# A hybrid encoder step on one core: another order of instructions in the attention step and in the opening

## The chip, the cores and the metric

The kernel runs on one core of one Trainium2 chip. The metric is the device time of one execution in microseconds (us). Before the change the median of three runs was 1349.14 us (1349.07 to 1354.99).

## What is computed

One layer of a streaming encoder, for a prompt of 1024 tokens and a running stream of 32 new tokens with 512 cached ones; the width is 1024, with 16 heads of 64. Everything is float32. Cut to what matters here:

```python
h = rmsnorm(x, norm_g)
q, k = rmsnorm(h @ Wq) * 64**-0.5, rmsnorm(h @ Wk)      # per head
v, logf = h @ Wv, log_sigmoid(h @ Wf + b_f)
u = (h @ Wua) * sigmoid(h @ Wub)
ga, gb, ma, mb = h @ Wga, h @ Wgb, h @ Wma, h @ Wmb
c = cumsum(logf)
p = softmax(where(causal, q @ k.T + c_q - c_k, -inf))   # per head, 128 queries at a time
o = p @ v
conv = causal_depthwise_conv(u, w_dw, 31 taps) + b_dw
ya = (o * silu(ga)) @ Wpa
yb = (silu(layernorm(conv)) * silu(gb)) @ Wpb
y = x + (sigmoid(ma) * ya + sigmoid(mb) * yb) @ Wout
```

Outputs are y, k, v, logf and the last 30 rows of u for both streams.

## The kernel before, in words

All data stands transposed: channels on the 128 partitions, the 1056 tokens along the free axis. A projection's output tile is 128 channels; its product runs over 8 k-tiles, in three chunks of 352 tokens. To keep float32 accuracy in 16-bit matmuls, the input and each weight tile are split into a high and a low part (`xh`, `xl`; `wh`, `wl`), and each product is three matmuls (`mms`, L183). Splitting a weight is: its squares for the scale on ACT (`stage`, L117), a sum over partitions on PE (`total`), a power of two (`power`), the high part on ACT (`high`, L138) and the low part on DVE in three pieces (`low`, L141). These jobs are due at fixed counts of `beat`, which is called once for each k-tile of a product (`begin`). A beat also adds `pace["rate"]` to a credit, from which the convolution's taps (`conv_taps`, L371, one DVE instruction over 1086 columns for each of 31 taps of 8 channel tiles) are issued.

**Opening** (`x_split`, L550 and after). The tokens come in three chunks of 256, 384 and 416. For each chunk and k-tile PE transposes the tokens (`ptx`, L576), ACT makes `xh` (L578) and DVE `xl` (L579). A table of jobs by k-tile says what else is issued there: squares of the next tokens, their roots (`rooted`, then `steps_of[...]`: two activations and a few small DVE operations), the scaling of the tokens (`scale`, L541 on DVE, L539 on GpSimd) and the parts of the first two weight tiles (`high(i, p)`, `low(i, p)`: part p of tile i). The products of the two tiles stand behind the transposes by a lag: `drain((2, 5))` in the first chunk, `drain((2, 2))` in the others.

**Attention.** A list `seq` holds 16 heads of 8 blocks (128 queries against all keys so far) and 4 `Sample` steps, one for four heads of the cached stream each. The step for element n in the loop at L1244 and after issues work of several elements:

- `scores` of n+3: two or four matmuls into PSUM (`psS`, L1121 and L1122; two buffers of two banks), then on DVE an add of the mask to the diagonal (L1124) and a maximum (`nm`, L1126).
- `turn` of n: the normalized weights `P` are transposed on PE (`ptr`, L1153) in groups of four into tiles of the pool `psT`, which has two buffers. The first group is copied out by ACT, the second (blocks 4 to 7) by DVE (`pt`, L1156).
- `soft` of n+3: the exponential on ACT (L1133), with its sum.
- `norm` of n+2: a reciprocal on DVE (L1138), then a scaling on GpSimd (L1139).
- `values` of n-2: with a head's last block 40 matmuls into two tiles of `psT` (`po`, L1172), copied and added into `ot` by ACT (L1176) and DVE (L1177, and L1179 with the gate `ga` for odd heads); for a `Sample` its own products.
- `fill(k)`: k steps of pending gate projections (`filler`), each the three matmuls of one k-tile, with a beat. There are 22 weight tiles of 24 steps, 528 steps in all.
- One step of `layernorm`, once the convolution's sums are there (`sides["ready"]`): sums over channels on PE into a tile of `psT` (`psn`, L1202), a scaling of the mean on ACT (L1211), the square of the mean (L1215) and three DVE operations (L1216 to L1218), later roots.

PE, SP, DVE and ACT keep the order in which the program issues here; only GpSimd is ordered by a planner. Loads of a head's `QA`, `QB`, `KA`, `KB` (L960 and after), of `ga` and of cache blocks go through SP's queue in that order too.

After the attention come the output products, which the change doesn't touch.

Of the kernel before, what the change touches and what calls it, by code (L numbers as in the profile page):

```python
# [8 lines left out]
F32 = mybir.dt.float32  # L9
# [5 lines left out]
ALU = mybir.AluOpType  # L15
AX = mybir.AxisListType

D = 1024
T = 1024
# [6 lines left out]
CH = 352  # L26
# [4 lines left out]
LNO = ((0,), (1, 2), (3,), (4, 5), (6,), (7,), ())  # L31
LNEXP = "natural_log_exp_and_others"
NFILL = 22
R_U, R_V, R_QK, R_G, R_A = 0.21, 0.18, 0.165, 0.23, 0.2
NWARM = 34
HT = TT // 2
HC = HT // 2
# [16 lines left out]
def build(tc, xT, xt, wv, wf, ckT, cv, clT, stT, vec, cst, yT, kT, vO, lfO, cpT, csT):  # L54
    nc = tc.nc
# [3 lines left out]
    def pool(name, bufs=1, stack=es, **kw):  # L59
        return stack.enter_context(tc.tile_pool(name=name, bufs=bufs, reuse_waits="tile", **kw))  # L60
# [19 lines left out]
    rstd = lnp.tile([128, TT], F32, name="rstd")  # L80
# [9 lines left out]
    class Batch:  # L90
# [46 lines left out]
        def high(self, i, wh, raw, ks):  # L137
            nc.scalar.mul(wh[:, ks, :], raw[:, ks, :], self.s[:, i:i + 1])  # L138

        def low(self, i, wl, wh, raw, ks):  # L140
            nc.vector.scalar_tensor_tensor(wl[:, ks, :], raw[:, ks, :], self.s[:, i:i + 1], wh[:, ks, :],  # L141
                                           op0=ALU.mult, op1=ALU.subtract)
# [35 lines left out]
    def mms(ps, w, rh, rl, sl, kts=range(KT), first=True, last=True):  # L178
        wh, wl = w[:2]
        n, N = 0, 3 * len(kts)  # L180
        for kt in kts:
            for a, b in ((wh, rh), (wl, rh), (wh, rl)):
                nc.tensor.matmul(ps, a[:, kt, :], b(kt, sl), start=(first and n == 0), stop=(last and n == N - 1))  # L183
                n += 1

    def csl(c):
        return slice(c * CH, (c + 1) * CH)
# [95 lines left out]
    class Banks:  # L283

        n = 0
# [101 lines left out]
    def pieces(o, n):  # L387

        if o + n <= T:
            return ((slice(0, n), slice(30 + o, 30 + o + n)),)  # L390
        return ((slice(0, T - o), slice(30 + o, 30 + T)), (slice(T - o, n), slice(60 + T, 60 + T + TS)))
# [134 lines left out]
    def root(t0, nt):  # L526

        rs = rs9[:, t0:t0 + nt]
        v, y = [xip.tile([128, 4], F32, name=f"n4{i}", tag=f"n4{i}", bufs=2)[:, :nt] for i in range(2)]
        nc.vector.tensor_scalar(v, rs, 1.0 / D, EPS, op0=ALU.mult, op1=ALU.add)  # L530
        nc.scalar.activation(y, v, AF.Ln)
        nc.scalar.activation(y, y, AF.Exp, scale=-0.5)
        return lambda: newton(rs, v, y)

    def scale(t, h, pool=False):
        r = rows(t)
        x, f = xtok[t][:r, half[h]], rs9[:r, t:t + 1]
        if pool:
            nc.gpsimd.tensor_scalar(x, x, f, 1.0, op0=ALU.mult, op1=ALU.mult)  # L539
        else:  # L540
            nc.vector.tensor_scalar(x, x, f, None, op0=ALU.mult)  # L541
# [3 lines left out]
    def drain(lags):  # L545
        for q, n in zip(behind, lags):
            while len(q) > n:
                q.pop(0)()

    def x_split(c, ws, u, jobs):  # L550


        o, n = XCH[c]
        sl = slice(o, o + n)
        pss = [pj.tile([128, 512], F32, name="pj", tag="pj") for _ in range(2)]

        def project(i, kt):
            mms(pss[i][:, :n], ws[i], X, XL, sl, range(kt, kt + 1), kt == 0, kt == KT - 1)
            if kt < KT - 1:
                return  # L560
            if i == 0:
                for a, b in pieces(o, n):
                    nc.scalar.mul(u[:, b], pss[0][:, a], recs[0].inv)
                return
            nc.vector.tensor_scalar(ua0[:, sl], pss[1][:, :n], recs[1].inv, None, op0=ALU.mult)
            if c == 2:
                for o2, n2, a2 in PCS:
                    b = slice(30 + o2, 30 + o2 + n2)
                    nc.scalar.activation(u[:, b], u[:, b], AF.Sigmoid)
                    nc.vector.tensor_mul(u[:, b], ua0[:, a2:a2 + n2], u[:, b])  # L570

        for kt in range(KT):
            pt = tr.tile([128, 512], F32, name="ptx", tag="tr") if kt % 3 == 2 else st.tile([128, 512], F32, name="ptx", tag="st")
            for j in range((n + 127) // 128):
                r = min(128, n - 128 * j)
                nc.tensor.transpose(pt[:, 128 * j:128 * j + r],  # L576
                                    xtok[o // 128 + j][:r, 128 * kt:128 * kt + 128], ident[:r, :r])
            nc.scalar.mul(xh[:, kt, sl], pt[:, :n], gs[:, kt:kt + 1])  # L578
            nc.vector.scalar_tensor_tensor(xl[:, kt, sl], pt[:, :n], gs[:, kt:kt + 1], xh[:, kt, sl],  # L579
                                           op0=ALU.mult, op1=ALU.subtract)  # L580
            for job in jobs.get(kt, ()):
                job()
            for i in range(2):
                behind[i].append(lambda i=i, kt=kt: project(i, kt))
            drain((2, 5 if c == 0 else 2))

    u0 = u_tile(0)
    ua0 = xip.tile([128, TT], F32, name="ua0")
# [13 lines left out]
    def known(i):  # L602
        recs[i].power(psq[:, i + 1:i + 2], 1)
# [19 lines left out]
    steps_of = {}  # L623

    def rooted(t0, nt):
        steps_of[t0] = root(t0, nt)
# [12 lines left out]
    for f in range(8):  # L639
# [16 lines left out]
        1: [lambda: squares(3)],  # L656
        2: [lambda: high(0, 1), lambda: low(0, 1)],
        3: [lambda: total(2), lambda: known(1), lambda: squares(4)],
        4: [lambda: high(1, 0), lambda: low(1, 0), lambda: rooted(2, 3), lambda: high(0, 2)],
        5: [lambda: steps_of[2](), lambda: scale(2, 0), lambda: scale(3, 0, True), lambda: scale(4, 0), lambda: low(0, 2)],  # L660
        6: [lambda: scale(3, 1, True), lambda: scale(2, 1), lambda: high(1, 1), lambda: low(1, 1)],
        7: [lambda: scale(4, 1), lambda: high(1, 2), lambda: low(1, 2)]})
    x_split(1, ws0, u0, {
# [73 lines left out]
    for c in range(4):  # L737
# [16 lines left out]
        for t in range(8):  # L754
            ps = pj.tile([128, 512], F32, name="pjv", tag="pj")
            n = 0
            for kt in range(KT):
                sl = slice(t * 128, t * 128 + 128)
# [243 lines left out]
    psT = pool("psT", 2, stack=p2, space=PS)  # L1002
# [4 lines left out]
    class Two:  # L1007
        n = 0
# [14 lines left out]
    def fill(n):  # L1023
        for _ in range(n):
            next(flow, None)
# [157 lines left out]
    seq = []  # L1183
# [12 lines left out]
    def pending(b):  # L1196
        return isinstance(b, Sample) or b.i % 2

    def over_channels(acc, put):
        for c in range(3):  # L1200
            pm = psT.tile([128, 512], F32, name="psn", tag="T")
            nc.tensor.matmul(pm[:, :CH], ones_f, acc[:, csl(c)], start=True, stop=True)  # L1202
            put(csl(c), pm[:, :CH])
            yield

    def layernorm():

        shift = sides["shift"]
        for _ in range(4):
            yield  # L1210
        yield from over_channels(mean, lambda sl, ps: nc.scalar.mul(mean[:, sl], ps, 1.0 / D))  # L1211

        def put(sl, ps):
            t = t352("t", 3)
            nc.scalar.activation(t, mean[:, sl], AF.Square)  # L1215
            nc.vector.scalar_tensor_tensor(rstd[:, sl], ps, 1.0 / D, t, op0=ALU.mult, op1=ALU.subtract)  # L1216
            nc.vector.tensor_add(mean[:, sl], mean[:, sl], shift[:, sl])
            nc.vector.tensor_scalar(rstd[:, sl], rstd[:, sl], EPS, None, op0=ALU.add)  # L1218

        yield from over_channels(rstd, put)  # L1220
        for c in range(6):
            sl = slice(c * CH // 2, c * CH // 2 + CH // 2)
            v, y = rstd[:, sl], t352("t", 3)[:, :CH // 2]
            nc.scalar.activation(y, v, AF.Ln)
            nc.scalar.activation(y, y, AF.Exp, scale=-0.5)
            yield
            w = t352("t", 3)[:, :CH // 2]
            nc.vector.tensor_copy(w, v)
            newton(v, w, y)
            yield  # L1230

    ones_f = cp.tile([128, 128], F32, name="ones_f", tag="ob")
# [5 lines left out]
    for n in range(3):  # L1238
# [3 lines left out]
            seq[n - 1].norm()  # L1242
        fill((8, 4, 0)[n])
    for n, b in enumerate(seq):  # L1244
        if n + 3 < len(seq):
            start(seq[n + 3])
        if n + 9 < len(seq) and getattr(seq[n + 9], "i", 1) == 0:
            seq[n + 9].head.load()
        if n + 6 < len(seq) and isinstance(seq[n + 6], Sample):
            seq[n + 6].load()  # L1250
        if getattr(b, "i", 0) == 3 and b.head.h + 1 < H:
            heads[b.head.h + 1].load_v()
        b.turn()
        if n + 3 < len(seq):
            seq[n + 3].soft()
        if n + 2 < len(seq):
            seq[n + 2].norm()
        some = 2 if isinstance(b, Sample) or b.i > 2 or b.head.h != 8 else 0
        fill(some)
        if n >= 2 and pending(seq[n - 2]):  # L1260
            seq[n - 2].values()
        fill(some)
        if n >= 3 and isinstance(seq[n - 3], Sample):
            seq[n - 3].finish()
        if "ready" in sides:
            next(ln, None)
# [17 lines left out]
    class Banks3:  # L1284
        n = 0
# [383 lines left out]
```

## Time and profile before

| what | value |
|---|---|
| median of three runs | 1349.14 us (1349.07 to 1354.99) |
| the profiled execution | 1345.89 us |
| its span, first to last instruction | 1344.1 us |
| granted TensorE clock in it, mean | 0.996 |
| PE idle in the first 60 us | 5.5 us |
| PE idle in the attention, 565.9 to 1052.6 us | 21.1 us |

The profile is of one execution. A row of a timeline gives start and duration in us, engine, line, operation, what it writes and reads, and in brackets the idle time of the engine before it with what ended it. A row of waits gives who waited for whom, the sum in us, how often, and the longest. A row of windows gives the stretch, its length and the busy time of PE, weight loads, DVE, ACT and GpSimd (POOL), each with its number of instructions, then the mean granted clock, the share of DMA and GB/s. A row of the chain gives start, length and what was on the path that ended last.

### The profile page before, as it was taken

The page shows a single profiled execution, that of the slowest core. Times are in us where ns is not written, and L with a number is a line of the kernel's source. Part 1 is how long each engine was busy: PE and PEld are TensorE (multiplying, and loading weights), DVE is VectorE, ACT ScalarE, POOL GpSimd, SP SyncE. Part 2 cuts the span into 40 slices and gives each one's busy share as a digit, 9 for nine tenths or more (in the row PEclk, how much of TensorE's full clock was granted, in tenths as well). Part 3 has the DMA queues.
Part 4 walks back from the last instruction along what each step waited for, and adds up shares of the span by engine and source line. Part 5 has one row for each costly group of instructions (what it writes and reads, how often), then busy time and mean ns, then how long its engine had stood idle before and what let it go on. Part 6 is the DMA issues. An engine that isn't in the chain of part 4 may idle for free.

```text
span 1344.1 us, 24837 instructions
## 1 busy us (share of the span) xinstructions
PE 1312.6 (98%) x9383; PEld 1003.1 (75%) x9383; DVE 990.4 (74%) x1532; ACT 719.0 (53%) x1362; POOL 505.8 (38%) x548
## 2 busy tenths in 40 slices
PE   8999999999999999999889998999999999999999
PEld 5687876666666666667567766777776699999998
DVE  6797879888999997987778866655554489166664
ACT  6644555757676743455555555655555566233320
POOL 2001124547484820243433442222222158255562
PEclk8999999999999999999999999999999999999999
DMA  6343233425352463535644643565452698544462
GB/s 251 98 140 104 93 112 118 139 82 187 95 180 87 162 166 109 160 90 155 165 109 123 186 132 99 147 179 132 131 152 54 240 313 262 176 128 146 142 190 69
DMA packets 113496, 194.97 MB, mean 145 GB/s; under 512 B 34080, under 2 KB 80032, under 8 KB 113376
## 3 DMA queue, kind: packets, MB, share of 16 engines
q1 hardware_dynamic: 113232, 193.31, 46.9%
q8 instruction: 74, 1.21, 0.4%
q14 instruction: 46, 0.38, 0.1%
q10 hardware_dynamic: 144, 0.07, 0.0%
HBM read 127.68 MB, written 65.64 MB: 144 GB/s over the span
## 4 chain that ended last, share of the span: by engine, by line
PE 82%; DVE 9%; ACT 3%; issue 2%; DMA 2%; SPq 1%; POOL 0%; DVEq 0%; ACTq 0%; POOLq 0%
PE pj L183 56%; PE pjv L761 6%; PE pj L1501 6%; PE po L1172 4%; PE ptr L1153 3%; DVE nm L1126 2%; DVE wl L141 2%; DVE y L371 2%; PE psS L1122 2%; PE psS L1121 2%; DMA ga<-s_ga 2%; ACT wh L138 1%; DVE psS L1124 1%; DMA s_q<-qh 1%; PE warm L477 1%
## 5 line engine op out<-in xcount | busy, mean ns | idle before, releaser
L183 PE MATMUL pj<-xh,wh 128*128 128x352 f16 (+2 forms) x1536 | 481.6, 314 | 2.3 <-ACT wh L138 1.4
L183 PE MATMUL pj<-xh,wl 128*128 128x352 f16 (+2 forms) x1536 | 481.2, 313 | 0.7 <-DVE wl L141 0.6
L183 PE MATMUL pj<-xl,wh 128*128 128x352 f16 (+2 forms) x1536 | 480.9, 313 | 0.5 <-DVE xl L579 0.4
L183 PEld LDWEIGHTS <-wh 128*128 128x128 f16 x3072 | 301.5, 98 | 162.1 <-issue 7.1
L371 DVE SCALAR_TENSOR_TENSOR y<-u,vec_t,y 128x1086 f32<-128x1086 f32 x240 | 346.8, 1446 | 12.0 <-ACT y L368 8.9
L1139 POOL TENSOR_SCALAR P<-P,nm 128x128 f32<-128x128 f32 (+7 forms) x128 | 129.9, 1015 | 279.9 <-DVE nm L1138 229.8
L183 PEld LDWEIGHTS <-wl 128*128 128x128 f16 x1536 | 150.5, 98 | 72.0 <-DVE wl L141 1.6
L141 DVE SCALAR_TENSOR_TENSOR wl<-raw,sc,wh 128x384 f16<-128x384 f32 (+1 forms) x192 | 128.2, 693 | 48.3 <-ACT wh L138 48.3
L1133 ACT ACTIVATE P<-psS,nm 128x128 f32<-128x128 f32 (+7 forms) x128 | 95.1, 743 | 113.3 <-DVE nm L1138 70.9
L1126 DVE TENSOR_REDUCE nm<-psS 128x1 f32<-128x128 f32 (+7 forms) x128 | 97.0, 758 | 12.5
L1153 PE MATMUL ptr<-ident,P 128*128 128x128 f32 x576 | 88.6, 276 | 17.3 <-DVE pt L1156 9.2
L175 POOL TENSOR_TENSOR wl<-raw,wh 128x384 fp32r<-128x384 f32 (+1 forms) x51 | 63.3, 1270 | 74.3 <-ACT wh L172 58.6
L1153 PEld LDWEIGHTS ptr<-ident,P 128*128 128x128 f32 x576 | 69.2, 141 | 28.2 <-DVE pt L1156 12.1
L1156 ACT COPY pt<-ptr 128x512 f32<-128x512 f32 (+3 forms) x128 | 64.3, 502 | 44.4 <-PE ptr L1153 43.2
L1121 PE MATMUL psS<-KB,QB 128*128 128x256 f32 (+2 forms) x192 | 81.8, 427 | 0.6 <-ACT P L1133 0.6
L880 POOL TENSOR_TENSOR sql<-sqf,sqh 128x352 fp32r<-128x352 f32 x48 | 57.0, 1187 | 65.8 <-ACT sqh L877 65.8
L138 ACT ACTIVATE wh<-raw,sc 128x1024 f16<-128x1024 f32 (+1 forms) x68 | 73.9, 1091 | 8.2 <-DVE sc L158 7.9
L1172 PE MATMUL po<-pt,V 128*64 128x256 f32 x640 | 72.8, 382 | 2.5 <-ACT pts L1078 1.7
L1124 DVE TENSOR_TENSOR psS<-psS,cmask 128x128 f32<-128x128 f32 x128 | 37.6, 294 | 46.0 <-PE psS L1122 45.6
L906 POOL TENSOR_TENSOR ql<-qn,qh 128x352 fp32r<-128x352 f32 (+1 forms) x48 | 67.8, 1429 | 6.6 <-ACT qh L905 6.5
L761 PE MATMUL pjv<-vwh,xh 128*128 128x260 f16 x256 | 70.1, 274 | 0.0
L761 PE MATMUL pjv<-vwl,xh 128*128 128x260 f16 x256 | 70.0, 273 | 0.0
(271 smaller groups left out, 2532.9 us busy)
## 6 DMA issues: line engine op xcount, KB each, us to landing
raw<-wf SPq DMA_DIRECT2D x92, 512.0 KB
QB<-s_q SPq DMA_DIRECT2D x32, 256.0 KB
KB<-s_k SPq DMA_DIRECT2D x32, 256.0 KB
kT<-qn SPq DMA_DIRECT2D x8, 528.0 KB
s_ga<-t SPq DMA_DIRECT2D x24, 176.0 KB
s_gb<-t SPq DMA_DIRECT2D x24, 176.0 KB
s_ma<-t SPq DMA_DIRECT2D x24, 176.0 KB
s_mb<-t SPq DMA_DIRECT2D x24, 176.0 KB
```

Source lines behind the costliest of these rows:

```text
L138: nc.scalar.mul(wh[:, ks, :], raw[:, ks, :], self.s[:, i:i + 1])
L141: nc.vector.scalar_tensor_tensor(wl[:, ks, :], raw[:, ks, :], self.s[:, i:i + 1], wh[:, ks, :], op0=ALU.mult, op1=ALU.subtract)
L183: nc.tensor.matmul(ps, a[:, kt, :], b(kt, sl), start=(first and n == 0), stop=(last and n == N - 1))
L371: t = nc.vector.scalar_tensor_tensor(y, u[:, i:i + CW], w, y, op0=ALU.mult, op1=ALU.add)
L761: nc.tensor.matmul(ps[:, :VC], a, b, start=(n == 0), stop=(n == 23))
L1121: nc.tensor.matmul(ps[:, b, :wm], QB[:, qsl], KB[:, ksl], start=True, stop=False)
L1126: nc.vector.tensor_reduce(nm[:, 0:1], ps[:, :nb, :w], axis=AX.XY, op=ALU.max, negate=True)
L1133: nc.scalar.activation(P[:, :nk].rearrange("p (b w) -> p b w", b=nb), ps[:, :nb, :w], AF.Exp, bias=nm[:, 0:1], accum_out=nm[:, 1:2])
L1139: nc.gpsimd.tensor_scalar(P[:, :nk], P[:, :nk], nm[:, 2:3], 1.0, op0=ALU.mult, op1=ALU.mult)
L1153: nc.tensor.transpose(pt[:, 128 * j:128 * j + 128], P[:, 128 * (4 * u + j):128 * (4 * u + j) + 128], ident)
L1172: nc.tensor.matmul(po[rows], V[:, j, :], parts[c][:, j, :], start=(c % 2 == 0 and j < 2), stop=(c % 2 == 1 and j >= 2 * c))
L1501: nc.tensor.matmul(pss[c][:, :HC], a[:, k, :], x, start=(not more and kt == 0 and n == 0), stop=(kt == 3 and n == 2), skip_group_check=more)
```

## The change

Five edits. The taps' rate in the attention goes from 0.2 to 0.165 a beat. In the opening the second tile's products lag seven k-tiles, and the jobs of k-tiles 4 and 5 change places. In `layernorm` the square of the mean is issued one step ahead of the matmul that it belongs to. In the attention's step `turn` of n and `norm` of n+2 come first, then the scores of n+3 and the loads, then the values of n-2, the exponential of n+3 and all fills together. The fills are four for each step, three at block 6 of heads 2 to 13; before, they were two and two around the values, and none at the first three blocks of head 8.

```diff
-R_U, R_V, R_QK, R_G, R_A = 0.21, 0.18, 0.165, 0.23, 0.2
+R_U, R_V, R_QK, R_G, R_A = 0.21, 0.18, 0.165, 0.23, 0.165
...
-            drain((2, 5 if c == 0 else 2))
+            drain((2, 7 if c == 0 else 2))
...
-        4: [lambda: high(1, 0), lambda: low(1, 0), lambda: rooted(2, 3), lambda: high(0, 2)],
-        5: [lambda: steps_of[2](), lambda: scale(2, 0), lambda: scale(3, 0, True), lambda: scale(4, 0), lambda: low(0, 2)],
+        4: [lambda: rooted(2, 3), lambda: high(0, 2), lambda: steps_of[2](), lambda: scale(2, 0), lambda: scale(3, 0, True)],
+        5: [lambda: scale(4, 0), lambda: high(1, 0), lambda: low(0, 2), lambda: low(1, 0)],
...
-        def put(sl, ps):
+        for c in range(3):
+            sl = csl(c)
             t = t352("t", 3)
             nc.scalar.activation(t, mean[:, sl], AF.Square)
-            nc.vector.scalar_tensor_tensor(rstd[:, sl], ps, 1.0 / D, t, op0=ALU.mult, op1=ALU.subtract)
+            yield
+            pm = psT.tile([128, 512], F32, name="psn", tag="T")
+            nc.tensor.matmul(pm[:, :CH], ones_f, rstd[:, sl], start=True, stop=True)
+            nc.vector.scalar_tensor_tensor(rstd[:, sl], pm[:, :CH], 1.0 / D, t, op0=ALU.mult, op1=ALU.subtract)
...
-        yield from over_channels(rstd, put)
...
     for n, b in enumerate(seq):
+        b.turn()
+        if n + 2 < len(seq):
+            seq[n + 2].norm()
         if n + 3 < len(seq):
             start(seq[n + 3])
...
-        b.turn()
+        if n >= 2 and pending(seq[n - 2]):
+            seq[n - 2].values()
         if n + 3 < len(seq):
             seq[n + 3].soft()
-        if n + 2 < len(seq):
-            seq[n + 2].norm()
-        some = 2 if isinstance(b, Sample) or b.i > 2 or b.head.h != 8 else 0
-        fill(some)
-        if n >= 2 and pending(seq[n - 2]):
-            seq[n - 2].values()
-        fill(some)
+        fill(3 if getattr(b, "i", 0) == 6 and 2 <= b.head.h < 14 else 4)
```

## The prediction, made before the result was known

> **What bounds the kernel now.** I read the page's engine line and the shares of its chain first, then busy time by stage, then who PE (the matmul engine) waited for in the attention, then single stretches of PE, DVE (VectorE) and ACT (ScalarE).
>
> ```profile
> PE 1312.6 (98%) x9383; PEld 1003.1 (75%) x9383; DVE 990.4 (74%) x1532; ACT 719.0 (53%) x1362; POOL 505.8 (38%) x548
> ...
> PE 82%; DVE 9%; ACT 3%; issue 2%; DMA 2%; SPq 1%; POOL 0%; DVEq 0%; ACTq 0%; POOLq 0%
> ```
> ```profile
> 0.00:20.00 20.00, 16.37 (x80) 10.19 (x81) 11.18 (x40) 13.42 (x30) 4.50 (x14) 0.83 0.94 348
> 20.00:60.00 40.00, 38.13 (x252) 24.94 (x251) 30.50 (x62) 24.77 (x45) 3.81 (x6) 1.00 0.30 102
> 565.90:820.00 254.10, 239.85 (x1777) 173.04 (x1777) 191.76 (x372) 142.75 (x308) 97.99 (x117) 1.00 0.50 136
> 820.00:1052.60 232.60, 225.71 (x1685) 163.36 (x1682) 132.51 (x325) 131.79 (x286) 56.55 (x100) 0.99 0.45 124
> 1052.60:1344.10 291.50, 287.47 (x1970) 279.51 (x1968) 177.06 (x227) 111.30 (x149) 149.68 (x120) 1.00 0.58 189
> ```
>
> PE bounds the kernel, and only 18% of the chain lies elsewhere. The rows give, after the stretch and its length, the busy time of PE, weight loads, DVE, ACT and POOL, then the clock and the DMA. The change touches two stages: the opening (PE idle 3.63 + 1.87 = 5.5 us in its first 60) and the attention, 565.9 to 1052.6, where PE idles 14.25 us while the conv taps run on DVE and 6.89 us afterwards. No part of the edit issues another matmul, so the gain can only come from these idles.
>
> ```profile
> PE ptr L1153 <- DVE pt L1156: 9.2, 11, 1.7
> PE ptr L1153 <- ACT pt L1156: 6.4, 5, 2.2
> PE po L1172 <- ACT pts L1078: 1.7, 2, 0.9
> PE ptr L1153 <- DVE ot L1177: 1.2, 1, 1.2
> PE po L1172 <- ACT mean L1211: 0.7, 1, 0.7
> PE psS L1121 <- ACT P L1133: 0.6, 2, 0.4
> PE psn L1202 <- ACT pt L1156: 0.6, 1, 0.6
> ```
> ```profile
> 964.37 4.54 PE L1172 MATMUL po<-pt,V 128*64 128x256 f32 x40
> 991.60 4.54 PE L1172 MATMUL po<-pt,V 128*64 128x256 f32 x40
> ```
> ```profile
> 911.54 0.22 PE ptr L1153 x2
> 911.76 1.79 PE pj L183 x12
> ...
> 947.88 0.23 PE psS L1121
> ...
> 1048.17 4.47 PE po L1172 x40
> ```
>
> These are all of PE's waits in the attention: 20.4 us in 23 waits, nearly all in front of transposes (ptr) whose PSUM buffer still has to be copied out by DVE or ACT. An undisturbed head lasts 991.60 - 964.37 = 27.23 us. A fill step is 1.79/4 = 0.45 us, a transpose 0.11, the scores of a block at most four times 0.24, a head's values 4.47. Sixteen such heads are 435.7 us; four cache blocks, reckoned as a head's eighth without values, (27.23 - 4.47)/8 = 2.8 each, bring 447. The stage lasts 486.7. So 39.6 us are over the undisturbed pace where 21.1 are shown idle: a wait costs more than its idle, since matmul rows overlap. The factor is between 1 and 1.9 (the cache blocks do more than I gave them); I take 1.5.
>
> **The opening.** Edits: roots and scales of tokens 256 to 639 move ahead of the second tile's first split (`high(1,0)`, `low(1,0)`); that tile's products lag 7 k-tiles instead of 5. Nothing is added.
>
> ```profile
> 16.33 0.39 PE L183 MATMUL pj<-xh,wh 128*128 128x256 f16 x1 [0.81 <-ACT wh L138]
> 16.98 0.39 PE L183 MATMUL pj<-xh,wl 128*128 128x256 f16 x1 [0.26 <-DVE wl L141]
> ...
> 21.86 0.55 PE L576 MATMUL ptx<-ident,xtok 128*128 128x128 f32 x3 [1.30 <-DVE xl L579]
> ```
> ```profile
> 16.31 0.62 DVE L141 SCALAR_TENSOR_TENSOR wl<-raw,sc,wh 128x384 f16<-128x384 f32 x1
> ...
> 19.26 1.33 DVE L541 TENSOR_SCALAR xtok<-xtok,rs 128x512 f32<-128x512 f32 x2
> 20.51 0.90 DVE L141 SCALAR_TENSOR_TENSOR wl<-raw,sc,wh 128x256 f16<-128x256 f32 x1
> 21.33 0.47 DVE L579 SCALAR_TENSOR_TENSOR xl<-ptx,gs,xh 128x256 f16<-128x256 f32 x1
> ```
>
> Three waits can go: 0.81 and 0.26 (the second tile's first products stand in front of its split) and 1.30 (the second chunk's first transpose waits for a residual behind scales and a split on DVE). After: the split of 16.31 leaves the front of the roots, so they run some 0.5 us earlier, but it returns between the same roots and the residual of 21.33; what falls is the stretch in which DVE waited on ACT. I get that residual done near 21.0 instead of 21.8, so the transpose starts 0.8 us earlier. Behind it six deferred products stand where four stood: two more groups of three matmuls at 0.11 us (1.79/12 scaled from 352 to 256 columns), 0.66 us; for the cover they give to late splits I credit 0.3, a choice. Net **-0.4 us**; bounds -2.4 (all three waits) and +0.7 (the products alone).
>
> **The layernorm.** The Square moves one step ahead of the matmul whose result it is subtracted from.
>
> ```profile
> 833.25 0.49 ACT L1215 ACTIVATE t<-mean 128x352 f32<-128x352 f32 x1
> ...
> 833.77 0.52 DVE L1216 SCALAR_TENSOR_TENSOR rstd<-psn,t 128x352 f32<-128x352 f32 x1 [0.21 <-ACT t L1215]
> ...
> 834.27 0.33 PE L1153 MATMUL ptr<-ident,P 128*128 128x128 f32 x1 [2.20 <-ACT pt L1156]
> ```
>
> The DVE evacuation at 833.77 waited for a Square that stood last in ACT's queue, and the transpose after it waited 2.20 us. Four waits lie in this stretch, head 8, whose first three blocks had no fills: 2.20, 1.2 (ot), 0.7 (mean) and 0.6 (psn), 4.7 together. After, the Square is a step old when its partner arrives, and every block has fills. Against it: the sums' matmul (psn) now stands straight before the transposes instead of before the scores, and takes one of their two buffers. I leave 1.7, so **-3.0**; bounds 0 and -4.7.
>
> **The step.** Transposes of block n come before scores of n+3; reciprocal and norm of n+2 before the add and reduce of n+3 on DVE; values before all four fills instead of in their middle. PE, DVE, ACT and SP keep program order here. SP's issues keep their mutual order (a cache block's turning passes the head loads, no transfer is added); the gate load (ga) still stands behind the eight loads of a head, so it is late as before.
>
> ```profile
> 585.03 1.23 DVE L1126 TENSOR_REDUCE nm<-psS 128x1 f32<-128x1024 f32 x1
> ...
> 588.64 0.62 DVE L141 SCALAR_TENSOR_TENSOR wl<-raw,sc,wh 128x384 f16<-128x384 f32 x1 [2.12 <-ACT wh L138]
> 589.18 1.34 DVE L371 SCALAR_TENSOR_TENSOR y<-u,vec_t,y 128x1086 f32<-128x1086 f32 x1
> 590.44 0.61 DVE L141 SCALAR_TENSOR_TENSOR wl<-raw,sc,wh 128x384 f16<-128x384 f32 x1
> ...
> 591.37 0.29 DVE L1126 TENSOR_REDUCE nm<-psS 128x1 f32<-128x128 f32 x1
> 591.57 0.41 DVE L1156 COPY pt<-ptr 128x256 f32<-128x256 f32 x1
> ```
> ```profile
> 586.37 1.12 ACT L1133 ACTIVATE P<-psS,nm 128x1024 f32<-128x1024 f32 x1 [1.03 <-DVE nm L1126]
> ...
> 587.48 1.14 ACT L138 ACTIVATE wh<-raw,sc 128x1024 f16<-128x1024 f32 x1
> ```
> ```profile
> 592.04 0.55 PE L1153 MATMUL ptr<-ident,P 128*128 128x128 f32 x3 [1.74 <-DVE pt L1156]
> ```
>
> This is the longest wait on a DVE copy. Read it backwards: the transpose at 592.04 needs the copy at 591.57; ahead of that stand the next block's reduce, a residual of a weight split, a tap and another residual, and the first residual idled 2.12 us for wh on ACT, which stood behind the exponential, which waited for the 1.23 us reduce.
>
> Two effects oppose each other. A copy no longer stands behind the add and reduce of its step: 0.6 us for a block of 128 keys, 1.5 for 1024, gained wherever DVE is simply behind (the two reduces above and an add that I take like the smaller). But that reduce, its exponential and what ACT does next start later, by the transposes and scores PE now does first. In a chain like the one above the slack of the next copy changes by reduce(n+4) - transposes(n) - scores(n+5): for n = 3, 1.5 - 4 x 0.11 - 0.24 (two matmuls of 256 columns) = +0.8; for n = 4 to 6, interpolating the reduce by keys, -0.2 to -0.4. The lower tap rate helps: 0.035 x 4 beats x 1.34 = 0.19 us less DVE work per block, 14 us over the 75 blocks that the taps last now, given back in some 20 later blocks where heads hardly wait. Of the 9.2 us I take a third off: **-3.1**; bounds +3 (n = 4 to 6 worse, eleven times 0.3) and -9.2. The ACT copies, 6.4 less the layernorm's 2.2, are 4.2: the fills after the values give DVE and ACT 0.9 us more to recover, the later exponential takes some back: **-1.2**; bounds +4 and -4.2. Scores waiting for an exponential (0.6) now stand behind the transposes: **-0.6**.
>
> Against: values follow transposes after scores (0.6 for a block of 640 keys) instead of two fills (0.9), so their cover falls by 0.3. The waits on pts grow by **+0.8**, the other heads' by **+0.7** (0 to 16 x 0.3 = 4.8). Twelve steps lose one fill, 0.45 us of cover before the eight transposes of block 7: **+0.5** (0 to 5.4). The fills are the same 528 in all.
>
> Sum of idle: -3.0 - 3.1 - 1.2 - 0.6 + 0.8 + 0.7 + 0.5 = -5.9; times 1.5, -8.9; with the opening -9.3. The profiled execution would fall from 1345.89 (span 1344.1, 1.8 us around it) to 1336.6. The median shown, 1349.14, lies 3.25 above that execution; I carry this over: **1340**.
>
> **Rivals.**
> Little gained: the late exponential eats what the earlier copies bring, only the layernorm (-3.0 x 1.5) and the opening stay: 1349.1 - 4.9 = 1344. For it: the chain at 592 is bound by ACT, not by DVE's backlog. Against it: DVE is busy 191.76 of 254.10 us while the taps run, so that backlog is common, and a copy that is issued earlier cuts it.
>
> Slower: the later reduce makes ACT's queue the bound. In order, the exponential of n+3 waits for that reduce, and wh, gate copies and the next block's copy stand behind it. It decides where reduce (1.5 with its add), exponential (1.1) and wh (1.1) together pass the time in which PE comes round, 27.23/8 = 3.4 us: for the longer blocks at a weight split, about 11 of the 22 splits. Each starts later by transposes and scores, up to 0.44 + 0.8; at half of that, 0.6, it is 6.6 us; 3.5 for values comes on top, the layernorm's 3.0 and the scores' 0.6 go off: +6.5 of idle, times 1.5, less 0.4, +9.4: 1358.5. Against it: psS has two buffers and norms two steps of lead, so lateness is mostly absorbed.
>
> Much faster: the tapped heads become like the tap-free ones, which idle 6.89 us after 820, less the layernorm's 1.2, 0.6 and 2.2 there, 2.9 for seven heads. Twice that for all, 5.8, leaves 15 of 20.4 to go, x 1.5 = 22 us: 1326. Against it: the splits stay.
>
> Colder opening: the clock was 0.83 over the first 20 us and 1.00 after, as if 20 x 0.17/0.5 = 7 us had run at half rate. If moving products out of that stretch keeps half rate for 3 us more, half of them is lost, +1.5 on whatever case holds. I give it 0.15; it decides nothing alone. The Trainium skill ("TensorE: Matmul & The Clock Gate", Part 1) speaks for it: the array runs at half rate until a free-running window of about 3.4 us was busy. By that page a thinner chunk could miss a window, an estimate of 1.7 us; the trace agrees in so far as its first 20 us are slow.
>
> **Chances.** Forecast 0.43, little gained 0.30, slower 0.13, much faster 0.14. The forecast's own range is 1335 to 1344. Over 0.5% (6.7 us, about what a measurement here tells from no change) means below 1342.4 or above 1355.9. Faster: 0.14 plus 0.38 of the forecast, 0.52. Within: 0.35. Slower: 0.13. The range takes in little gained and most of much faster, and reaches up over the copies' and values' upper bounds: 1328 to 1351, with some 0.2 outside.
>
> **What would show it.** Right: PE's waits on DVE copies fall to about 6 us and none lies behind a reduce of its own step; no wait over 1 us beside the layernorm sums; scores never wait for P; the second chunk's first transpose starts near 21. Wrong: waits on ACT copies at blocks 4 to 6 grow, values wait in most heads, or the slow clock lasts beyond 20 us.

## The result, and the profile after

The changed kernel takes 1368.43 us (median of four runs, 1367.82 to 1370.17) against 1351.52 for the kernel before, run beside it (1349.07 to 1354.99). The ratio is 1.0127 [1.0101, 1.0153]: slower by 17 us. The forecast was 1340, faster. The profiled execution took 1367.89 us, 22.0 more than the profiled one of before; that one, at 1345.89, was below every timed run of the kernel before, so the pair of profiles shows some 5 us more loss than the medians.

First the same parts of the page as before: the engines' busy time, then the shares of the chain.

```profile
PE 1321.9 (97%) x9383; PEld 995.0 (73%) x9383; DVE 991.1 (73%) x1532; ACT 714.1 (52%) x1362; POOL 474.0 (35%) x548
...
PE 78%; DVE 7%; DMA 5%; ACT 4%; issue 3%; SPq 2%; POOL 0%; ACTq 0%; DVEq 0%; POOLq 0%
```

Every engine has as many instructions as before, DVE and ACT are busy for nearly the same time and GpSimd for less: no work came in. PE's share of the chain fell from 82% to 78%, and that of DMA rose from 2% to 5%. One load does come later to its user: DVE waits 19.9 us for the gate `ga` (L1179) in the attention, against 9.9 before. But e2 below, which loses 14 us, has 6.6 us of this wait, and e4, which is faster than the kernel before, has 17.7; so it isn't what costs the time. What PE has more in busy time (9.3 us) is no work either: part of it is matmuls at half clock, told of in the last section.

Next, where the time lies. These rows are from the chain of after and then from that of before: a run of matmuls ahead of the attention and the long run that follows it, with start and length.

```profile
534.98 21.50 PE pj L183 x144
...
1074.69 200.94 PE pj L183 x1272
```
```profile
534.35 21.50 PE pj L183 x144
...
1052.64 201.18 PE pj L183 x1272
```

The stretch itself is unchanged; it starts 22.05 us later. The run of 144 matmuls started at 534.35 before, so the opening and the projections account for 0.6 and the attention for 21.4. The busy time by stage (same columns as before the change):

```profile
0.00:20.00 20.00, 15.24 (x75) 9.23 (x75) 11.90 (x41) 14.06 (x31) 5.64 (x15) 0.91 0.93 342
20.00:60.00 40.00, 39.19 (x251) 26.01 (x252) 28.80 (x60) 23.49 (x40) 2.67 (x4) 0.96 0.30 99
565.00:820.00 255.00, 237.29 (x1715) 164.05 (x1713) 182.67 (x355) 133.79 (x293) 64.02 (x109) 0.98 0.47 126
820.00:1052.60 232.60, 219.21 (x1623) 151.83 (x1622) 135.28 (x326) 127.11 (x286) 57.76 (x107) 1.00 0.48 130
```

PE now idles 17.7 us in the stretch up to 820, in which nearly all taps of the attention run, and 13.4 in the one behind it (14.25 and 6.89 before). The last tap starts at 835.86, before at 772.68. So the loss isn't tied to the taps. PE's waits in the attention of after, as sum, times and longest (four rows left out hold 3.4 together):

```profile
PE ptr L1153 <- ACT pt L1156: 16.0, 17, 2.4
PE po L1172 <- ACT pts L1078: 7.1, 4, 2.3
PE ptr L1153 <- DVE os_t L1102: 2.6, 2, 1.8
PE ptr L1153 <- ACT mean L1211: 2.3, 2, 1.3
PE ptr L1153 <- DVE pt L1156: 1.6, 3, 1.1
```

The waits on DVE's copies did go, 9.2 to 1.6. In their place stand waits on ACT's copies, 6.4 to 16.0, and on the copies of the four `Sample` steps in front of a head's values (`pts`), 1.7 to 7.1. The sum rose from 20.4 to 33.0.

Now ACT's own waits in the attention, before and then after. The exponential (L1133) waits for its reduce (`nm`); the copy (L1156) waits for its transposes. The reciprocal (L1138) that some rows name comes right behind the reduce on DVE and is issued behind that exponential before the change, so I read these rows as waits for the reduce too.

```profile
ACT P L1133 <- DVE nm L1138: 70.9, 62, 3.1
ACT pt L1156 <- PE ptr L1153: 43.2, 50, 2.1
ACT P L1133 <- DVE nm L1126: 38.4, 30, 3.3
```
```profile
ACT P L1133 <- DVE nm L1126: 124.4, 79, 5.0
...
ACT pt L1156 <- PE ptr L1153: 10.7, 16, 2.0
```

The second kind of row tells whether ACT is on time: where it waits for the transposes, it was there before them. That happened 50 times before and 16 times after. The first kind tells what ACT did instead: it stood at an exponential whose reduce had not come, 109.3 us before, 124.4 after, up to 5.0 us in one piece, with the copy behind it in the same queue. These rows leave out exponentials whose wait is put down to something else. The page's line for the exponential has all idle time ahead of it, behind the busy time and the mean (before, then after):

```profile
L1133 ACT ACTIVATE P<-psS,nm 128x128 f32<-128x128 f32 (+7 forms) x128 | 95.1, 743 | 113.3 <-DVE nm L1138 70.9
```
```profile
L1133 ACT ACTIVATE P<-psS,nm 128x128 f32<-128x128 f32 (+7 forms) x128 | 95.0, 742 | 154.5 <-DVE nm L1126 124.4
```

So the exponentials' waits grew by 41 us, with the same work.

The longest wait shows this in one place, the last head's blocks of 512 and 640 keys. ACT copies the first group of each (1052.32 and 1057.25), and between them stands the exponential of a block of 896 keys. ACT, then DVE, then PE of after:

```profile
1052.32 0.59 ACT L1156 COPY pt<-ptr 128x512 f32<-128x512 f32 x1 [0.61 <-PE ptr L1153]
1054.68 1.01 ACT L1133 ACTIVATE P<-psS,nm 128x896 f32<-128x896 f32 x1 [1.78 <-DVE nm L1126]
...
1055.68 1.14 ACT L138 ACTIVATE wh<-raw,sc 128x1024 f16<-128x1024 f32 x1
...
1057.25 0.58 ACT L1156 COPY pt<-ptr 128x512 f32<-128x512 f32 x1
```
```profile
1053.48 1.09 DVE L1126 TENSOR_REDUCE nm<-psS 128x1 f32<-128x896 f32 x1
```
```profile
1054.86 0.60 PE L1153 MATMUL ptr<-ident,P 128*128 128x128 f32 x4
1057.89 0.44 PE L1153 MATMUL ptr<-ident,P 128*128 128x128 f32 x1 [2.43 <-ACT pt L1156]
```

And ACT, DVE and PE of before at the same place:

```profile
1034.10 0.58 ACT L1156 COPY pt<-ptr 128x512 f32<-128x512 f32 x1 [1.64 <-PE ptr L1153]
1035.18 1.01 ACT L1133 ACTIVATE P<-psS,nm 128x896 f32<-128x896 f32 x1 [0.49 <-DVE nm L1138]
...
1037.75 0.58 ACT L1156 COPY pt<-ptr 128x512 f32<-128x512 f32 x1
```
```profile
1034.00 1.09 DVE L1126 TENSOR_REDUCE nm<-psS 128x1 f32<-128x896 f32 x1
```
```profile
1036.74 0.60 PE L1153 MATMUL ptr<-ident,P 128*128 128x128 f32 x4
1038.39 0.33 PE L1153 MATMUL ptr<-ident,P 128*128 128x128 f32 x1 [1.04 <-ACT pt L1156]
```

Between the two copies ACT does the same work in both kernels. Before, the reduce started 0.10 us ahead of the first copy, now 1.16 behind it, since the transposes come ahead of the scores; so the exponential starts 2.36 us behind the first copy instead of 1.08, and the second copy 4.93 instead of 3.65. PE has its four transposes done and waits for that copy: 2.43 us instead of 1.04.

### The profile page after: what moved, and what is told of

It is laid out like the page before. It is cut to its first block, busy times and chain, and to the rows that moved or that the text cites. A ratio compares the mean times of both kernels' runs of the same rounds, so it can differ in the third digit from the quotient of the medians.

```text
span 1366.1 us, 24780 instructions
## 1 busy us (share of the span) xinstructions
PE 1321.9 (97%) x9383; PEld 995.0 (73%) x9383; DVE 991.1 (73%) x1532; ACT 714.1 (52%) x1362; POOL 474.0 (35%) x548
## 4 chain that ended last, share of the span: by engine, by line
PE 78%; DVE 7%; DMA 5%; ACT 4%; issue 3%; SPq 2%; POOL 0%; ACTq 0%; DVEq 0%; POOLq 0%
PE pj L183 54%; PE pjv L761 6%; PE pj L1501 5%; PE po L1172 4%; PE ptr L1153 3%; DVE nm L1126 2%; DMA ga<-s_ga 2%; PE psS L1122 2%; PE psS L1121 2%; DVE y L371 1%; ACT P L1133 1%; DVE wl L141 1%; ACT wh L138 1%; DMA s_y<-y 1%; DMA pf<-s_cs 1%
## 5 line engine op out<-in xcount | busy, mean ns | idle before, releaser
L1139 POOL TENSOR_SCALAR P<-P,nm 128x128 f32<-128x128 f32 (+7 forms) x128 | 95.8, 748 | 295.0 <-DVE nm L1138 284.0
L1133 ACT ACTIVATE P<-psS,nm 128x128 f32<-128x128 f32 (+7 forms) x128 | 95.0, 742 | 154.5 <-DVE nm L1126 124.4
L138 ACT ACTIVATE wh<-raw,sc 128x1024 f16<-128x1024 f32 (+2 forms) x68 | 73.9, 1091 | 8.1 <-DVE sc L158 7.8
L1121 PE MATMUL psS<-KB,QB 128*128 128x256 f32 (+2 forms) x192 | 76.9, 402 | 0.0
L761 PE MATMUL pjv<-vwh,xl 128*128 128x260 f16 x256 | 69.9, 273 | 0.0
L1156 ACT COPY pt<-ptr 128x512 f32<-128x512 f32 (+3 forms) x128 | 64.1, 501 | 11.0 <-PE ptr L1153 10.7
L1172 PEld LDWEIGHTS po<-pt,V 128*64 128x64 f32 x640 | 44.9, 139 | 34.0 <-ACT pts L1078 8.8
```

The costliest lines, as they stand in the source:

```text
L761: nc.tensor.matmul(ps[:, :VC], a, b, start=(n == 0), stop=(n == 23))
L1121: nc.tensor.matmul(ps[:, b, :wm], QB[:, qsl], KB[:, ksl], start=True, stop=False)
L1133: nc.scalar.activation(P[:, :nk].rearrange("p (b w) -> p b w", b=nb), ps[:, :nb, :w], AF.Exp, bias=nm[:, 0:1], accum_out=nm[:, 1:2])
L1139: nc.gpsimd.tensor_scalar(P[:, :nk], P[:, :nk], nm[:, 2:3], 1.0, op0=ALU.mult, op1=ALU.mult)
L1172: nc.tensor.matmul(po[rows], V[:, j, :], parts[c][:, j, :], start=(c % 2 == 0 and j < 2), stop=(c % 2 == 1 and j >= 2 * c))
```

## The experiments

My theory after the result: putting the transposes first makes the reduce and the exponential late, and what stands behind the exponential in ACT's queue, copies of transposes among it, becomes late with it; putting the values first takes two fills of cover from their buffers. The rivals: the layernorm, the lower tap rate, the fills or the opening cost something instead; the earlier reciprocal on DVE blocks that queue; the loss is the clock. Ratios are to the kernel before run beside each.

| kernel | median us | ratio [95%] |
|---|---|---|
| e1 all but the step's order | 1340.87 | 0.9934 [0.9914, 0.9954] |
| e2 transposes and norm first, alone | 1364.16 | 1.0103 [1.0087, 1.0119] |
| e3 values first, alone | 1358.62 | 1.0063 [1.0045, 1.0082] |
| e13 values behind exponential and norm, ahead of the fills | 1356.40 | 1.0054 [1.0034, 1.0073] |
| e12 the change, norm behind the exponential again | 1365.83 | 1.0125 [1.0108, 1.0142] |
| e5 opening alone | 1349.65 | 1.0006 [0.9997, 1.0015] |
| e8 tap rate alone | 1345.18 | 0.9971 [0.9961, 0.9982] |
| e9 layernorm alone | 1345.68 | 0.9969 [0.9958, 0.9981] |
| e10 fills alone | 1345.95 | 0.9973 [0.9963, 0.9983] |
| e4 the change, exponential a step later | 1338.33 | 0.9909 [0.9889, 0.9929] |
| e14 as e4, norm between the fills | 1336.47 | 0.9911 [0.9896, 0.9926] |
| e11 as e4, with the old order of the rest | 1333.44 | 0.9887 [0.9872, 0.9902] |

**e1: the step's order undone, the rest of the change kept.** Against the changed kernel:

```diff
-        b.turn()
-        if n + 2 < len(seq):
-            seq[n + 2].norm()
         if n + 3 < len(seq):
             start(seq[n + 3])
...
-        if n >= 2 and pending(seq[n - 2]):
-            seq[n - 2].values()
+        b.turn()
         if n + 3 < len(seq):
             seq[n + 3].soft()
-        fill(3 if getattr(b, "i", 0) == 6 and 2 <= b.head.h < 14 else 4)
+        if n + 2 < len(seq):
+            seq[n + 2].norm()
+        fill(2)
+        if n >= 2 and pending(seq[n - 2]):
+            seq[n - 2].values()
+        fill(1 if getattr(b, "i", 0) == 6 and 2 <= b.head.h < 14 else 2)
```

> The changed kernel with the step's order of before (scores, transposes, exponential, norm, two fills, values, the rest of the fills); rate, opening, layernorm and the twelve short steps stay changed. Late-exponential theory (the reduce and exponential of n+3 start only after the transposes, so ACT's copies come late): the loss sits in the step, so this is 1346 to 1354 us, with PE's waits for ACT copies back near 6 us. Rival, cover (values and short steps lose fills): some of the loss stays through the short steps, 1354 to 1360. Rival, rate and layernorm (taps and sums now fall on later heads): 1360 or more.

Measured 0.9934, 9 us faster than before and better than the 1346 to 1354 us that I expected. The order alone therefore costs 1.0127 - 0.9934 = 1.9%, some 26 us, more than the whole loss, and the rest of the change is a gain. ACT waits for transposes 64 times in it, 55.9 us: it is on time again, and PE's waits on its copies are 3.1 us.

**e2: of the step, only transposes and norm moved first, on the kernel before.**

```diff
     for n, b in enumerate(seq):
+        b.turn()
+        if n + 2 < len(seq):
+            seq[n + 2].norm()
         if n + 3 < len(seq):
             start(seq[n + 3])
...
-        b.turn()
         if n + 3 < len(seq):
             seq[n + 3].soft()
-        if n + 2 < len(seq):
-            seq[n + 2].norm()
```

> The kernel before with transposes and norm moved first in the step and nothing else; values stay between two fills and two. Late-exponential theory: it carries most of the loss, +9 to +16 us over before, PE's waits for ACT copies 13 us or more, those for DVE copies under 3. Cover theory: -4 to +4 us.

Measured 14 us slower, within what was expected. Of ACT's waits in it:

```profile
ACT P L1133 <- DVE nm L1126: 140.1, 89, 3.7
...
ACT pt L1156 <- PE ptr L1153: 10.4, 13, 2.0
```

This part alone makes ACT late: 13 copies on time, and PE's waits on them rise from 6.4 to 14.7 us, while those on DVE's copies fall from 9.2 to 1.8.

**e3: only the values moved ahead, on the kernel before; e13: the same, but behind the exponential.** In both the values lose the two fills that stood ahead of them.

e3 first:

```diff
         b.turn()
+        if n >= 2 and pending(seq[n - 2]):
+            seq[n - 2].values()
         if n + 3 < len(seq):
             seq[n + 3].soft()
...
         fill(some)
-        if n >= 2 and pending(seq[n - 2]):
-            seq[n - 2].values()
         fill(some)
```

Then e13:

```diff
         some = 2 if isinstance(b, Sample) or b.i > 2 or b.head.h != 8 else 0
+        if n >= 2 and pending(seq[n - 2]):
+            seq[n - 2].values()
         fill(some)
-        if n >= 2 and pending(seq[n - 2]):
-            seq[n - 2].values()
         fill(some)
```

> The kernel before with values moved ahead of the exponential and of all four fills and nothing else; scores still come before transposes. Late-exponential theory: +2 to +7 us, almost all of it values waiting for pts. Cover theory: +9 to +16 us.

> The kernel before with values ahead of all fills but behind exponential and norm: e3 with only the exponential's place put back. If e3 lost its 9 us because the exponential stands behind ACT's copies of the values, this is -2 to +3 us against before. If it lost them because values have two fills less of cover, it stays at +6 to +10.

Measured 8.5 and 7.3 us slower by the ratios; the intervals overlap. The 8.5 lies between the two ranges that I gave for e3, so e3 alone decides nothing. With the values behind the exponential nearly all of the loss stays, so it is the cover. Of PE's waits, three rows of e3 that grew most (before they were 1.7 and twice nothing; in e13 the first is 4.9):

```profile
PE po L1172 <- ACT pts L1078: 5.0, 4, 1.9
PE po L1172 <- ACT pt L1156: 1.7, 4, 1.2
PE ptr L1153 <- POOL P L1139: 1.4, 2, 1.2
```

**e12: the changed kernel with the norm back behind the exponential.**

```diff
         b.turn()
-        if n + 2 < len(seq):
-            seq[n + 2].norm()
...
             seq[n + 3].soft()
+        if n + 2 < len(seq):
+            seq[n + 2].norm()
```

> The changed kernel with the norm of n+2 put back behind the exponential of n+3. Late-exponential theory: the reduce of n+3 is late because its scores come after the transposes, whatever stands before it on DVE, so 1364 to 1370 as changed. Rival, reciprocal: the reduce is late because the reciprocal of n+2 ahead of it waits for ACT; then 1345 to 1357.

Measured 1.0125, as the change itself. The reciprocal's place is not the cause.

**e5, e8, e9, e10: the other parts one by one, on the kernel before.** e5 has the two opening edits, e8 the line with `R_A` = 0.165, e9 the new `layernorm`, e10 the fills:

```diff
-        some = 2 if isinstance(b, Sample) or b.i > 2 or b.head.h != 8 else 0
-        fill(some)
+        some = 1 if getattr(b, "i", 0) == 6 and 2 <= b.head.h < 14 else 2
+        fill(2)
```

> The kernel before with the two edits of the opening alone. As the prediction had it: -0.4 us, between -2.4 and +0.7. Clock rival: the first transposes of the second chunk come about 1 us earlier, and where half rate then covers the deferred products the gain is taken back, so -0.5 to +1.5 us with its sign changing from run to run.

> The kernel before with the taps' rate 0.165 alone. The old step's share of the whole edit's 9 us gain is sought. If less DVE work per block is what helps, -3 to -6 us and the waits for DVE copies fall to 6 us or less; if the taps only move to later heads, -1 to +1.

> The kernel before with the layernorm's squares one step earlier alone. The prediction gave this and the fills of head 8 together -3.0 us of idle, -4.5 of time. Alone: -1 to -4, and the 2.2 us wait behind a square goes. Rival: the wait only passes to another releaser, -0.5 to +0.5.

> The kernel before with the fills of head 8 given back and one taken from block 6 of heads 2 to 13, the rest untouched. If head 8 without fills was what let PE run into ACT and DVE, -2 to -4 us; if the short steps cost their cover (0.45 us each), +1 to +4.

The opening is worth nothing that can be measured. The other three bring 3.6 to 4.2 us each, 12 together, of which e1 with all of them has 9; the intervals allow for that. Most of it is not fewer waits: the mean granted clock over their runs was 0.9959, 0.9958 and 0.9961 against 0.9938 for the kernel before, and 0.002 of 1349 is some 2.8 us. The traces show no gain in the attention: from the run of 144 matmuls to the long run it lasts 517.5, 518.7 and 518.5 us in e8, e9 and e10, against 518.3 in the profile of before, and PE's waits in it sum to 20.1, 19.7 and 20.9 against 20.4. The sign that I gave for the tap rate, waits on DVE's copies of 6 us or less, didn't come: e8 has 8.2. None of these parts costs anything that can be measured, so none explains the result.

**e4: the changed kernel with the exponential one step later.** The scores and the reduce of n+3 stay where the change puts them; the exponential is that of n+2, right behind the transposes, so its reduce was issued a whole step before. The loop ahead of the attention issues two exponentials instead of three.

```diff
         b.turn()
         if n + 2 < len(seq):
-            seq[n + 2].norm()
+            seq[n + 2].soft()
         if n + 3 < len(seq):
             start(seq[n + 3])
...
-        if n + 3 < len(seq):
-            seq[n + 3].soft()
         fill(3 if getattr(b, "i", 0) == 6 and 2 <= b.head.h < 14 else 4)
+        if n + 2 < len(seq):
+            seq[n + 2].norm()
```

> The changed kernel with the exponential taken off the place that it waits in: that of n+2 is issued right behind the transposes of n, one step after its scores, and the norm of n+2 at the step's end. If ACT's queue held up by an exponential that waits for its reduce is the cause, the waits for ACT copies fall under 6 us, the waits for pts under 3, and the time is 1345 to 1355. If cover is the cause, the waits for pts stay at 5 to 7 us and the time at 1360 or more.

Measured 0.9909: 2.2%, some 29 us, less than the changed kernel, and better than I expected. ACT's waits in it:

```profile
ACT pt L1156 <- PE ptr L1153: 93.3, 84, 2.6
ACT P L1133 <- DVE nm L1126: 0.6, 1, 0.6
```

The exponential doesn't wait any more (154.5 to 1.1 us by the page's line), and ACT is ahead of the transposes 84 times instead of 16. PE's waits on ACT's copies are 2.0 us, and those on `pts` 1.8.

**e14: as e4, the norm between the fills; e11: the late exponential with scores ahead of transposes and the values between the fills, as before.** Both diffs are against e4, e14 first:

```diff
-        fill(3 if getattr(b, "i", 0) == 6 and 2 <= b.head.h < 14 else 4)
+        fill(2)
         if n + 2 < len(seq):
             seq[n + 2].norm()
+        fill(1 if getattr(b, "i", 0) == 6 and 2 <= b.head.h < 14 else 2)
```

And e11:

```diff
+        if n + 3 < len(seq):
+            start(seq[n + 3])
         b.turn()
         if n + 2 < len(seq):
             seq[n + 2].soft()
-        if n + 3 < len(seq):
-            start(seq[n + 3])
...
+        fill(2)
         if n >= 2 and pending(seq[n - 2]):
             seq[n - 2].values()
-        fill(3 if getattr(b, "i", 0) == 6 and 2 <= b.head.h < 14 else 4)
+        fill(1 if getattr(b, "i", 0) == 6 and 2 <= b.head.h < 14 else 2)
```

> e4 with the norm of n+2 issued after two fills instead of at the step's end. In e4 PE waits 4.6 us for GpSimd's scaling (8 waits); an earlier norm should take 3 to 4 of them away: 1333 to 1337. If the reciprocal then waits for the exponential and holds up DVE, 1338 to 1342.

> The exponential one step later, as in e4, but with scores before transposes and values between the fills as before the change; the rest of the change kept. If a blocked exponential is all that makes the order of scores and transposes matter, this lies within 3 us of e4 (1336 to 1341). If transposes first is worth something of itself once the exponential is out of the way, it is 3 to 8 us slower than e4.

e14 can't be told from e4 by the ratios; its waits on GpSimd's scaling fell from 4.6 to 2.7 us, about half of what I expected. e11 is the fastest of all, 15 us under the kernel before and some 6 under e1 by the ratios. It lies below the 1336 to 1341 us that I gave it, and is not slower than e4, as the rival had it. One row of ACT's waits, and then the first of PE's, in e11:

```profile
ACT pt L1156 <- PE ptr L1153: 120.0, 115, 2.4
```
```profile
PE ptr L1153 <- POOL P L1139: 2.9, 4, 1.2
```

ACT waits for transposes 115 times, and PE's waits on ACT's copies are 2.0 us. What is left to PE is first GpSimd's scaling (`P`, L1139), which now follows its exponential within one step. With the early exponential the two orders lie 26 us apart (e1 against the change); with the late one 0.9909 against 0.9887, about 3, with intervals that overlap. So nearly all that the new order cost was paid through the exponential's place in ACT's queue.

## Why the prediction was wrong

**The step that failed** is the ACT-copies term of "The step": "the fills after the values give DVE and ACT 0.9 us more to recover, the later exponential takes some back: -1.2; bounds +4 and -4.2". It measured +9.6 (6.4 to 16.0, with the layernorm's 2.2 counted in; 1.2 more in front of L1080), outside the bounds. I had the mechanism in the text, as the slack that "changes by reduce(n+4) - transposes(n) - scores(n+5)", and priced it on a DVE copy with -0.2 to -0.4 a block. But the later exponential acts on every block and on ACT's queue, and the row that says how close ACT already was to its copies, 50 waits for transposes in 128 blocks, I had not read. e2 has this part alone: +14 us. e4 and e11 take the wait away and the loss with it.

**The DVE copies** (-3.1, bounds +3 and -9.2) had the right sign and more than twice the size: -7.6. A copy issued ahead of its step's reduce was on time (1.8 us in e2 too). But it wasn't the only way: in e11 the copy stands behind the reduce as in e1, the exponential comes a step later (and the norm behind the fills), and these waits are 0.9 us against e1's 9.2. So they, too, came mainly through the exponential, as in the chain at 592, where DVE idled for a `wh` that stood behind it. ACT's copies took more than all of the gain back.

**The values** (+0.8 for `pts`, +0.7 for other heads, bound 4.8) were too small: `pts` alone grew by 5.4, at the four `Sample` steps. I counted the cover as falling by 0.3 us, since the scores stand ahead of the values now. In e3, where no scores stand between and all of the two fills' 0.9 us are gone, `pts` is 5.0. In the changed kernel it is 7.1 although less cover is gone, since ACT is later there: e2, which leaves the values between the fills, has 3.1, and e4, with the values as early as in the change but the exponential a step later, 1.8. At one of the `Sample` steps ACT's copy stands behind an exponential, a weight split and two steps of the layernorm's roots (ACT in the changed kernel):

```profile
916.29 0.58 ACT L1133 ACTIVATE P<-psS,nm 128x384 f32<-128x384 f32 x1 [1.40 <-PE ptr L1077]
...
916.86 1.14 ACT L138 ACTIVATE wh<-raw,sc 128x1024 f16<-128x1024 f32 x1
...
918.52 0.57 ACT L1078 COPY pts<-ptr 128x512 f32<-128x512 f32 x1
```

PE's values start at 919.14 behind 2.29 us of idle.

**The layernorm and the fills of head 8** (-3.0, times 1.5 is -4.5): e9 and e10 gained 4.2 and 3.6, together 7.8, most of it with a higher clock. Right in sign; that they gain by the four waits I named is not shown: in e9 the wait of 2.20 us is gone (the longest on ACT's copies is 1.0), but a new one of 2.6 us on `rstd` (L1220) has come. I had also read that wait too narrowly. What the transpose at 834.27 waited for is ACT's copy, and ahead of it stand not only the Square of 0.49 us but, among others, an exponential and a weight split (ACT in the kernel before):

```profile
830.78 1.01 ACT L1133 ACTIVATE P<-psS,nm 128x896 f32<-128x896 f32 x1 [2.26 <-DVE nm L1138]
...
833.64 0.58 ACT L1156 COPY pt<-ptr 128x512 f32<-128x512 f32 x1
```

The row that I took for the layernorm's already showed the mechanism that failed. The lower tap rate, which I let count only within the step, gained 3.9 (e8), most of that too with a higher clock; and I let the taps last to 820, where the last stands at 772.68.

**The factor 1.5** from idle to time was about right, in this pair of executions. The waits rose by 12.6, the attention by 21.4; 5.1 of that is clock (below), and (21.4 - 5.1)/12.6 is 1.3.

**The opening** (-0.4, bounds -2.4 and +0.7). The second chunk's first transpose was forecast "near 21" and starts at 20.67, but a new wait of 1.42 us on a residual stands ahead of it, and the deferred products behind it run at half clock for 2.5 us. PE in the changed kernel:

```profile
20.27 0.38 PE L183 MATMUL pj<-xh,wl 128*128 128x256 f16 x1 [1.42 <-DVE wl L141]
...
20.67 0.90 PE L576 MATMUL ptx<-ident,xtok 128*128 128x128 f32 x3
21.36 0.42 PE L183 MATMUL pj<-xh,wh 128*128 128x256 f16 x1
21.57 0.42 PE L183 MATMUL pj<-xh,wl 128*128 128x256 f16 x1
```

Products start 0.21 apart here and 0.11 from 23.84 on. The clock was 0.91 over the first 20 us and 0.96 over the next 40, against 0.83 and 1.00: 20 x 0.09 + 40 x 0.04 = 3.4 us lost, as much as 20 x 0.17 before. So the slow clock did last beyond 20 us, but the total didn't change, nor did PE's idle in the first 60 us, 5.6 against 5.5: the waits only changed places. e5 measured nothing.

**The rivals.** "Slower" was the one that came true, with its mechanism: "the exponential of n+3 waits for that reduce, and wh, gate copies and the next block's copy stand behind it". Its price (+9.4) was half the result's. I confined it to "about 11 of the 22 splits" and set against it that "lateness is mostly absorbed"; the buffers of psS absorb a late exponential, not the copy that is queued behind it. Of the signs that the text gave for being wrong, two appeared, the waits on ACT's copies and the slow clock beyond 20 us; values waited at the four `Sample` steps only, not in most heads. Some signs for being right appeared as well: few waits on DVE's copies, no scores waiting for `P`, the first transpose near 21. They show that the waits the text watched went, not that the time did. One step went unpriced: the text called the gate load "late as before", and DVE's wait for it doubled, though the runs don't show it to cost time.

**Left open.** Order edits alone sum to 14 + 8.5 = 22.5 us, the order within the change costs 26; the difference lies within the intervals. How much of the gain of e8 to e10 comes from the clock alone and how much from their waits, I can't separate. Part of the clock isn't their doing: the opening, which e9 and e10 leave as it was, had a clock of 0.96 and 0.94 over its first 20 us in their profiles, against 0.83 before. Other mixtures for the opening weren't tried.

## What to carry to other kernels

Before an instruction is moved, ask for every in-order queue which instruction in it will wait for the moved one, and what unrelated work stands behind that waiter; here one exponential, waiting for a reduce, held up the copies on which the bounding engine depends. A wait of an engine off the critical path is harmless only as long as that engine still arrives early at its next hand-over: count how often it waits there for the bounding engine (here 115 and 84 times in e11 and e4, 50 before, 16 in the changed kernel and 13 in e2). The remedy for such a queue is to issue the consumer a step later, when its input is already there, rather than the producer earlier.

## What the runs showed of the hardware

Short waits can cost clock as well. Busy time by stretches of 5 us in the changed kernel, with the granted clock behind the five engines:

```profile
590.00:595.00 5.00, 3.28 (x20) 1.97 (x18) 4.55 (x9) 2.17 (x6) 1.12 (x1) 0.88 0.10 36
595.00:600.00 5.00, 5.00 (x30) 3.32 (x29) 4.30 (x11) 2.52 (x5) 0.86 (x2) 0.78 0.16 44
665.00:670.00 5.00, 5.00 (x34) 3.00 (x32) 1.42 (x3) 0.58 (x1) 1.58 (x6) 0.66 1.03 218
685.00:690.00 5.00, 5.00 (x24) 3.20 (x23) 4.00 (x8) 2.03 (x4) 1.01 (x1) 0.66 0.01 2
1055.00:1060.00 5.00, 2.57 (x11) 1.62 (x10) 1.73 (x5) 2.83 (x6) 1.01 (x1) 0.80 0.10 36
1060.00:1065.00 5.00, 5.00 (x33) 3.40 (x32) 2.71 (x6) 2.84 (x4) 1.12 (x1) 0.86 0.01 2
```

Four places lose 1.7 us each (5 x 0.34; 5 x (0.12 + 0.22); 5 x (0.20 + 0.14)), 6.8 together, against one such place before. Each is 3.4 us at half rate: behind the 2.43 us wait at 1057.89, products start 0.29 apart up to 1061.32 and 0.15 from then on. The Trainium skill ("TensorE: Matmul & The Clock Gate", Part 1) says that the rate is set by whether a free-running window of about 3.4 us was busy; these lengths agree. What stood ahead of the four was 0.58 and 1.14 us of idle close together, and single waits of 2.27, 1.99 and 2.43 us; ahead of the one before the change, 1.25 and 0.57. That so little idle in the midst of dense work is enough I had not expected, nor that it isn't always: 2.29 us ahead of 919.14 left the clock at 1.00. The slower kernels have more such places in the attention: four in e2 and e12, three in e3 and e13, of which one is twice as long; e1, e8, e9 and e10 have one or two, e4, e11 and e14 one or none. Of the 21.4 us that the attention lost in this pair of executions, 5.1 are this. The profiled execution of before had a clock of 0.996, though, where 25 later runs of that kernel had 0.9938 on average; 0.0022 of 1344 is 3 us, so against a usual execution the clock's part is nearer 2 us. Either way the loss isn't the clock.
